# The end of a decoder layer: final norm with its weights multiplied in early, four roots at once and one correction for the last rows

## The chip, the cores and the metric

One core of a Trainium2 chip runs the whole program. The metric is the device time in microseconds, the median of several runs. All engines (PE the matmuls, DVE VectorE, ACT ScalarE, POOL GpSimd, SP which issues transfers) work through their own instruction queues in order and wait for one another by semaphores.

## What is computed

One layer of a decoder trunk over 1024 tokens of width 1024: three mixers of the tokens merged under gates, then a two-layer MLP, then a final RMS norm. The change lies in the last lines, after the second MLP product:

```python
def rms_norm(x, g):
    x32 = x.astype(jnp.float32)
    y = x32 * lax.rsqrt(jnp.mean(x32 * x32, axis=-1, keepdims=True) + EPS)
    return (y * g.astype(jnp.float32)).astype(x.dtype)
...
        hn = rms_norm(h, norm_mlp_g[l])
        up = jax.nn.relu(jnp.einsum('bsd,df->bsf', hn, w_mlp_up[l]))
        h = h + jnp.einsum('bsf,fd->bsd', up * up, w_mlp_down[l])
    return rms_norm(h, final_norm_g)
```

## The kernel before

The tokens lie in eight row chunks `H[0]` to `H[7]` of 128 rows and 1024 columns (tiles `a` in the profile); a chunk has two halves of 512 columns, `hsl(0)` and `hsl(1)`. The second MLP product is computed by a seven-product scheme: for each of `NJ` slices of the hidden width there are seven bursts `i` = 0 to 6, and each burst has four products `p` = 0 to 3 of 12 matmuls (float32 operands split in a high and a low part). `dn_product(n, p)` issues one product and its eviction (L1617): DVE adds the result in PSUM to a half of `H[c]`. In a slice, bursts 3 to 6 accumulate into the same four PSUM banks (`aux2`), so a product's partial sums are evicted four times. Which half is meant goes by the burst: `i` = 3 the left halves of `H[0..3]`, 4 their right halves, 5 the right halves of `H[4..7]`, 6 the left halves of `H[4..7]`.

The order of the instructions on each engine is the order in which the code is written (a manual schedule). Between the products `advance(dn)` issues a step that splits operands of a later burst: a cast on ACT (L132) and a subtraction on DVE (L133). The last such step stands behind product 2 of burst 4 of the last slice.

In the last slice (`final`) the norm is woven in from burst 3 on. Every evicted half is squared and summed by ACT (L1822) into a column `fs`. With burst 5 the rows `H[p]`, complete by then, get their root from `rsqrt_col` (L107 to L112: a first guess by integer arithmetic and three corrections, nine column operations on DVE, behind the addition L1787), and one DVE instruction (L1827) scales a whole row chunk by root and weights `fg`; SP sends it out in two halves. The right halves of `H[4..7]` are multiplied by the weights (L1825). With burst 6 the left halves are multiplied by the weights, on POOL for `p` < 3 and on DVE for the last (L1832); root and scaling of a chunk follow one product later: both halves by ACT (L1799, L1795), of the last chunk one by DVE (L1802). All output transfers are issued by SP (L1783).

Of the kernel before, what the change touches and what calls it, by code (L numbers as in the profile page):

```python
# [11 lines left out]
AF = mybir.ActivationFunctionType  # L12
ALU = mybir.AluOpType
# [3 lines left out]
P = 128  # L17
T = 1024
D = 1024
KD = D // P  # L20
NCH = T // P
HF = 512
EPS = 1e-6
# [13 lines left out]
def trunk_kernel(ctx: ExitStack, tc: tile.TileContext, x, norm_mix_g, w_in, b_gate, gmlp_ln_g, gmlp_ln_b,  # L37
# [4 lines left out]
    nc = tc.nc  # L42
    x, w_in, b_gate, out = x[0], w_in[0], b_gate[0], out[0]
# [24 lines left out]
    def nm(s):  # L68
        uid[0] += 1
        return f"{s}_{uid[0]}"  # L70

    def act(shape=(P, T), dt=F32):
        return pools[0].tile(list(shape), dt, tag="act", name=nm("a"))
# [7 lines left out]
    def sm(n, tag, dt=F32, bufs=None):  # L81
        return small.tile([P, n], dt, tag=tag, name=nm(tag), bufs=bufs)
# [3 lines left out]
    tt = nc.vector.tensor_tensor  # L86
    stt = nc.vector.scalar_tensor_tensor
    ts = nc.vector.tensor_scalar
    actv = nc.scalar.activation
    mm = nc.tensor.matmul  # L90

    def hsl(h):
        return slice(h * HF, h * HF + HF)
# [11 lines left out]
    def rsqrt_col(dst, v, scale, e):  # L105
        nh, r, q = sm(1, "rsq_v", bufs=2), sm(1, "rsq_r", bufs=2), sm(1, "rsq_q", bufs=2)
        ts(out=r, in0=v, scalar1=scale, scalar2=e, op0=ALU.mult, op1=ALU.add)  # L107
        ts(out=nh, in0=r, scalar1=-0.5, scalar2=None, op0=ALU.mult)
        ts(out=r.bitcast(I32), in0=r.bitcast(I32), scalar1=-0.5, scalar2=float(0x5F3759DF), op0=ALU.mult, op1=ALU.add)
        for i in range(3):  # L110
            stt(out=q, in0=r, scalar=nh, in1=r, op0=ALU.mult, op1=ALU.mult)  # L111
            stt(out=(dst if i == 2 else r), in0=q, scalar=1.5, in1=r, op0=ALU.add, op1=ALU.mult)  # L112
# [172 lines left out]
    with tc.manual_schedule():  # L285
# [29 lines left out]
        ss, rs = sm(NCH, "ss"), sm(NCH, "rsx")  # L315
# [8 lines left out]
        def row_scale(c, pool=False):  # L324
            if pool:
                nc.gpsimd.tensor_scalar(out=rows[c], in0=rows[c], scalar1=rs[:, c:c + 1], scalar2=0.0, op0=ALU.mult, op1=ALU.add)
            else:
                ts(out=rows[c], in0=rows[c], scalar1=rs[:, c:c + 1], scalar2=None, op0=ALU.mult)
# [13 lines left out]
        row_sum(0)  # L342
        row_root(0, 1)
        row_scale(0)
        wv0 = v_weights(0, (0,))
        xt[0] = transpose_rows(rows[0])
# [4 lines left out]
        x_low(xt[0], 0, 0)  # L351
        x_high(xt[0], 0, 1)
        row_scale(1)
        x_low(xt[0], 0, 1)
        v_start(0, range(0, 4))
# [9 lines left out]
        x_low(xt[1], 1, 0)  # L365
        row_root(2, 3)
        row_scale(2)
        x_low(xt[1], 1, 1)
        row_root(3, 4)
# [170 lines left out]
    queue, ready, pending = [], [], []  # L540
# [515 lines left out]
    for c in range(NCH):  # L1056
# [5 lines left out]
        rs = sm(1, "lrs")  # L1062
# [305 lines left out]
    H = []  # L1368
# [20 lines left out]
    with tc.manual_schedule():  # L1389
        for cp in range(NCH // 2):  # L1390
# [15 lines left out]
            for i in range(2):  # L1406
                h = H[2 * cp + i]
# [194 lines left out]
    def dn_product(n, p):  # L1602
        j, i = divmod(n, 7)
        if i < 3:
            if i == 0:
                main[j, "b2", p] = aux()
            ps = main[j, "b2", p] if i < 2 else aux()
        else:
            if i == 3:
                main[j, p] = aux2()  # L1610
            ps = main[j, p]
        u, w = OPS[n]
        lhs = [[u[part][kk][:, p * P:(p + 1) * P] for kk in range(4)] for part in range(2)]
        seventh(ps, lhs, w, i in (0, 2, 3))
        c, nb = {0: (p + 4, 1), 1: (p, 1), 2: (p, 0), 3: (p, 0), 4: (p, 1), 5: (p + 4, 1), 6: (p + 4, 0)}[i]
        h = H[c][:, hsl(nb)]
        tt(out=h, in0=ps, in1=h, op=ALU.add)  # L1617
        return c, nb

    def advance(gen):  # L1620
        next(gen, None)
# [23 lines left out]
    with tc.manual_schedule():  # L1645
# [125 lines left out]
        H = [None] * NCH  # L1771
        for c in (4, 5, 6, 7, 0, 1, 2, 3):
            H[c] = act()
            nc.scalar.dma_start(out=H[c], in_=h_d[c])
            if c == 7:
                dn_product(0, 0)
                prev.p4()
                prev.last_sum()
        sums, scaled = {}, {}
        roots = sm(NCH, "roots")  # L1780

        def out_row(c, nb, o):
            nc.sync.dma_start(out=out[c * P:(c + 1) * P, hsl(nb)], in_=o)  # L1783

        def row_scale(c):
            rs = roots[:, c:c + 1]
            tt(out=sums[c, 0], in0=sums[c, 0], in1=sums[c, 1], op=ALU.add)  # L1787
            rsqrt_col(rs, sums[c, 0], 1.0 / D, EPS)
            return rs

        def last_rows(c, rs, left):
            o = scaled[c]
            left(o[:, hsl(0)], rs)
            out_row(c, 0, o[:, hsl(0)])
            actv(o[:, hsl(1)], o[:, hsl(1)], AF.Identity, scale=rs)  # L1795
            out_row(c, 1, o[:, hsl(1)])

        def by_scalar(o, rs):
            actv(o, o, AF.Identity, scale=rs)  # L1799

        def by_vector(o, rs):
            ts(out=o, in0=o, scalar1=rs, scalar2=None, op0=ALU.mult)  # L1802

        waiting = None
        for n in range(NB):
            j, i = divmod(n, 7)
            final = j == NJ - 1
            if final and i == 3:
                fg = act()
                nc.scalar.dma_start(out=fg, in_=final_norm_g.partition_broadcast(P))  # L1810
            for p in range(NCH // 2):
                if n + p == 0:
                    continue
                c, nb = dn_product(n, p)
                advance(dn)
                if final and i == 3:
                    advance(dn)
                if not final or i < 3:
                    continue
                h = H[c][:, hsl(nb)]  # L1820
                sums[c, nb] = sm(1, f"fs{c}{nb}")
                actv(act()[:, :HF], h, AF.Square, accum_out=sums[c, nb])  # L1822
                if i == 5:
                    scaled[c] = act()
                    tt(out=scaled[c][:, hsl(1)], in0=h, in1=fg[:, hsl(1)], op=ALU.mult)  # L1825
                    rs, o = row_scale(p), act()
                    stt(out=o, in0=H[p], scalar=rs, in1=fg, op0=ALU.mult, op1=ALU.mult)  # L1827
                    for b in range(2):
                        out_row(p, b, o[:, hsl(b)])
                elif i == 6:  # L1830
                    eng = nc.gpsimd if p < 3 else nc.vector
                    eng.tensor_tensor(out=scaled[c][:, hsl(0)], in0=h, in1=fg[:, hsl(0)], op=ALU.mult)  # L1832
                    if waiting is not None:
                        last_rows(waiting, row_scale(waiting), by_scalar)
                    waiting = c
        last_rows(waiting, row_scale(waiting), by_vector)
# [1 line left out]
_INS = ['x', 'norm_mix_g', 'w_in', 'b_gate', 'gmlp_ln_g', 'gmlp_ln_b', 'gmlp_w_s', 'gmlp_b_s', 'lru_conv_w',  # L1838
        'lru_conv_b', 'lru_w_r', 'lru_b_r', 'lru_w_i', 'lru_b_i', 'lru_lambda', 'ssd_conv_w', 'ssd_conv_b',
# [25 lines left out]
```

## Time and profile before

| | |
|---|---|
| median of 3 runs | 1958.79 us (1957.18 to 1960.37) |
| span of the profiled execution | 1959.5 us (no separate time is given for it; the span is 0.7 us above the median) |
| granted TensorE clock, mean | 0.991 |
| PE busy | 1905.2 us, 97% |
| DVE busy | 1410.2 us, 72% |
| ACT busy | 1014.1 us, 52% |
| POOL busy | 259.3 us, 13% |

A line of the timeline has the start in us, the duration, the engine, the line of the kernel, the operation, output <- inputs, shapes and count; in square brackets stands how long the engine sat idle before it and what ended that. A line of groups has the busy time, then the mean ns of one. In the rows of groups and of the timeline buffer numbers are left out, so `a<-a,a` can be three tiles. Ends of matmuls are modelled.

### The profile page before, as it was taken

What the parts mean: (1) busy time and instruction counts of PE and PEld (TensorE: products, weight loads), DVE (VectorE), ACT (ScalarE), POOL (GpSimd) and SP (SyncE); (2) the same over time, 40 slices, a digit from 0 to 9 for tenths busy, and PEclk for the clock granted to TensorE, in tenths of its full rate; (3) what the DMA queues carried; (4) which work ended last, traced back from release to release, by engine and by line L of the source; (5) the groups of instructions that cost most, each with busy time, mean ns of one, the idle gap of its engine ahead of it and who ended that gap; (6) DMA issues with size and microseconds to landing.
All of it is one profiled execution on the core that took longest, in us unless ns stands there. A gap on an engine that the chain in (4) does not pass through costs nothing.

```text
span 1959.5 us, 23757 instructions
## 1 busy us (share of the span) xinstructions
PE 1905.2 (97%) x8928; PEld 1587.5 (81%) x8928; DVE 1410.2 (72%) x2039; ACT 1014.1 (52%) x1471; POOL 259.3 (13%) x355
## 2 busy tenths in 40 slices
PE   8999999999999999999999999998999999999996
PEld 7998878888887787878778887877788887888885
DVE  6585869788758767677777888248655567688787
ACT  6435959676534545454554544167555556243253
POOL 3112112122342010100010110000211110000000
PEclk9999999999999999999999999999999999999998
DMA  4346475576754343434497986331544448453532
GB/s 162 75 137 145 110 153 122 121 164 138 169 142 136 107 151 108 151 108 129 149 287 256 279 220 194 107 108 54 199 139 167 154 172 294 164 172 118 183 119 86
DMA packets 211015, 301.25 MB, mean 154 GB/s; under 512 B 13028, under 2 KB 125876, under 8 KB 210900
## 3 DMA queue, kind: packets, MB, share of 16 engines
q1 hardware_dynamic: 167348, 158.54, 26.4%
q0 software_dynamic: 34544, 119.69, 22.8%
q10 hardware_dynamic: 9008, 21.51, 3.1%
q8 instruction: 70, 1.15, 0.3%
q14 instruction: 45, 0.37, 0.1%
HBM read 195.75 MB, written 74.58 MB: 138 GB/s over the span
## 4 chain that ended last, share of the span: by engine, by line
PE 74%; DVE 9%; issue 6%; ACT 5%; DMA 5%; POOL 1%; ACTq 0%; POOLq 0%; DVEq 0%; SPq 0%
PE aux L487 39%; PE ps L564 14%; PE gps L487 10%; PE aux L257 4%; PE aux L1387 2%; PE aux L800 1%; DMA a<-acs_d 1%; DMA c<-yc_d 1%; ACT a L1436 1%; DMA raw<-in_w_in_dram 1%; PE aux L736 1%; PE aux L732 1%; DVE a L133 1%; DVE rsq_q L111 1%; ACT a L132 1%
## 5 line engine op out<-in xcount | busy, mean ns | idle before, releaser
L564 PE MATMUL ps<-xn,wh 128*128 128x512 f32 x1088 | 295.0, 392 | 0.0
L487 PE MATMUL aux<-b,b 128*128 128x512 f32 x1152 | 264.4, 389 | 1.0 <-DVE b L133 0.9
L487 PEld LDWEIGHTS aux<-b,b 128*128 128x128 f32 x1152 | 216.0, 188 | 47.0 <-DVE b L133 1.8
L564 PEld LDWEIGHTS ps<-xn,wh 128*128 128x128 f32 x1088 | 202.9, 188 | 42.2 <-issue 0.9
L487 PE MATMUL aux<-a,b 128*128 128x512 f32 x960 | 219.4, 389 | 0.0
L487 PEld LDWEIGHTS aux<-a,b 128*128 128x128 f32 x960 | 180.2, 188 | 37.4
L564 PE MATMUL ps<-xn,wl 128*128 128x512 f32 x544 | 168.2, 389 | 0.0
L487 PE MATMUL gps<-xn,wt 128*128 128x512 f32 x684 | 160.2, 392 | 2.1 <-DVE a L238 2.1
L487 PE MATMUL aux<-b,wt 128*128 128x512 f32 x672 | 156.9, 389 | 0.0
L487 PEld LDWEIGHTS gps<-xn,wt 128*128 128x128 f32 x684 | 129.4, 189 | 29.5 <-issue 2.5
L487 PEld LDWEIGHTS aux<-b,wt 128*128 128x128 f32 x672 | 126.1, 188 | 26.2
L132 ACT ACTIVATE b<-wt 128x1024 fp32r<-128x1024 f32 x88 | 90.8, 1052 | 86.4 <-DMA wt<-u_d 51.9
L133 DVE TENSOR_TENSOR wt<-a,wt 128x1024 fp32r<-128x1024 f32 x66 | 80.8, 1225 | 66.9 <-ACT wt L132 66.9
L564 PEld LDWEIGHTS ps<-xn,wl 128*128 128x128 f32 x544 | 102.1, 188 | 21.4
L133 DVE TENSOR_TENSOR b<-wt,b 128x1024 fp32r<-128x1024 f32 x88 | 107.1, 1218 | 15.8 <-ACT b L132 15.8
L1617 DVE TENSOR_TENSOR a<-aux,a 128x512 f32<-128x512 f32 x112 | 76.9, 687 | 50.2 <-PE aux L487 50.2
L133 DVE TENSOR_TENSOR a<-a,a 128x1024 fp32r<-128x1024 f32 (+1 forms) x68 | 66.6, 985 | 41.5 <-ACT a L132 41.5
L133 DVE TENSOR_TENSOR wt<-rt,wt 128x1024 fp32r<-128x1024 f32 x35 | 42.8, 1224 | 57.2 <-ACT wt L132 57.0
L132 ACT ACTIVATE a<-a 128x1024 fp32r<-128x1024 f32 (+1 forms) x68 | 55.9, 837 | 54.1 <-DVE a L1569 45.9
L487 PE MATMUL aux<-a,wt 128*128 128x512 f32 x336 | 78.7, 390 | 3.3 <-ACT a L1494 3.3
L487 PEld LDWEIGHTS aux<-a,wt 128*128 128x128 f32 x336 | 62.9, 188 | 17.2 <-ACT a L1494 4.2
L132 ACT ACTIVATE wt<-a 128x1024 fp32r<-128x1024 f32 x66 | 69.6, 1055 | 8.7 <-DVE a L515 8.3
(349 smaller groups left out, 3521.2 us busy)
## 6 DMA issues: line engine op xcount, KB each, us to landing
wt<-u_d SPq DMA_DIRECT2D x54, 512.0 KB
u_d<-a POOLq DMA_DIRECT2D x48, 512.0 KB, 5.3
raw<-in_w_in_dram SPq DMA_DIRECT2D x34, 512.0 KB
wl<-raw POOLq DMA_DIRECT2D x34, 512.0 KB, 5.1
g_d<-a POOLq DMA_DIRECT2D x24, 512.0 KB, 3.3
a<-g_d ACTq DMA_DIRECT2D x24, 512.0 KB
rt<-in_w_in_dram SPq DMA_DIRECT2D x19, 512.0 KB
a<-in_w_in_dram SPq DMA_DIRECT2D x19, 512.0 KB
```

The lines of the kernel that those rows point to most:

```text
L111: stt(out=q, in0=r, scalar=nh, in1=r, op0=ALU.mult, op1=ALU.mult)
L132: actv(dst_hi, src, AF.Copy)
L133: (eng or nc.vector).tensor_tensor(out=dst_lo, in0=src, in1=dst_hi.bitcast(F32), op=ALU.subtract)
L257: mm(ps[:, :nt], X.tok(a, k, c), wk[k][w], start=(k == 0 and i == 0), stop=(k == KD - 1 and i == 2))
L487: mm(ps, lhs[l][kk], rhs[r][kk], start=(new and n == 0), stop=(n == 11), skip_group_check=not new)
L564: mm(ps[:, hsl(h)], w[wi][:, k, :], a.rhs(ai, k, h), start=(n == 0), stop=(n == 3 * KD - 1))
L732: mm(yo[:, tok(i)], pv[c // 2][:, c % 2, j * P:(j + 1) * P], Cf[:, tok(c)], start=True, stop=True)
L736: mm(yi[64 * h:64 * h + 64, tok(i)], xdt[c // 2][:, c % 2, 2 * j + h, :], E[c // 2][:, c % 2, 2 * j + h, :], start=True, stop=True)
L800: mm(ps, w[wi][:, q * P:(q + 1) * P], S["xs"][half][ai], start=(n == 0), stop=(n == 2))
L1387: mm(ps, M.tok(a, k, c), wo[nb][k][w], start=(k == 0 and a + w == 0), stop=(k == KD - 1 and a == 1))
L1436: actv(Nf[th, k // 2][:, k % 2, (c % 4) * P:(c % 4 + 1) * P], ps[:, i * P:(i + 1) * P], AF.Identity, scale=g2c[:, KD + k:KD + k + 1])
L1617: tt(out=h, in0=ps, in1=h, op=ALU.add)
```

## The change

The weights are multiplied into the rows `H[0..3]` on DVE during burst 4 (`weigh`, L1790 of the new code), and into both halves of `H[4..7]` during bursts 5 and 6, all on DVE; POOL has no part in it any more. With the first product of burst 5 the roots of the four chunks `H[0..3]` are found together on 4 columns: mean (L1806, L1807), square root by ACT (L1808), then reciprocal and one correction by DVE (L1811 to L1815); ACT scales each chunk whole (L1802) and SP sends it in one transfer of 512 KB. For `H[4..7]`, the sum of squares of the half known first is turned into a bias column `known` (L1857); ACT takes the root of the other half's sum plus this bias (L1819), and DVE makes the reciprocal and one correction (L1823 to L1827). DVE scales the left half (L1795) and ACT the right (L1797), one product later. The very last transfer is issued by ACT.

```diff
+        def square_sum(c, nb):
+            actv(act()[:, :HF], H[c][:, hsl(nb)], AF.Square, accum_out=squares[c // half][nb][:, c % half:c % half + 1])
+        def weigh(c, nb):
...
+            tt(out=scaled[c][:, hsl(nb)], in0=H[c][:, hsl(nb)], in1=fg[:, hsl(nb)], op=ALU.mult)
+        def out_half(c, nb, eng, queue):
+            o, rs = scaled[c][:, hsl(nb)], root[:, c % half:c % half + 1]
+            if eng is nc.vector:
+                ts(out=o, in0=o, scalar1=rs, scalar2=None, op0=ALU.mult)
+            else:
+                actv(o, o, AF.Identity, scale=rs)
+            queue.dma_start(out=out[c * P:(c + 1) * P, hsl(nb)], in_=o)
+        def rows_first(p):
+            o = scaled[p]
+            actv(o, o, AF.Identity, scale=root[:, p:p + 1])
+            nc.sync.dma_start(out=out[p * P:(p + 1) * P, :], in_=o)
+        def roots_first():
+            tt(out=mean, in0=squares[0][0], in1=squares[0][1], op=ALU.add)
+            ts(out=mean, in0=mean, scalar1=1.0 / D, scalar2=EPS, op0=ALU.mult, op1=ALU.add)
+            actv(root, mean, AF.Sqrt)
+        def refine_first():
+            nc.vector.reciprocal(out=root, in_=root)
+            tt(out=step_, in0=root, in1=root, op=ALU.mult)
+            tt(out=step_, in0=step_, in1=mean, op=ALU.mult)
+            ts(out=step_, in0=step_, scalar1=-0.5, scalar2=1.5, op0=ALU.mult, op1=ALU.add)
+            tt(out=root, in0=root, in1=step_, op=ALU.mult)
+        def root_last(p):
+            q = slice(p, p + 1)
+            actv(root[:, q], squares[1][0][:, q], AF.Sqrt, scale=1.0 / D, bias=known[:, q])
+        def refine_last(p):
+            q = slice(p, p + 1)
+            stt(out=mean[:, q], in0=squares[1][0][:, q], scalar=1.0 / D, in1=known[:, q], op0=ALU.mult, op1=ALU.add)
+            ts(out=mean[:, q], in0=mean[:, q], scalar1=-0.5, scalar2=None, op0=ALU.mult)
+            nc.vector.reciprocal(out=root[:, q], in_=root[:, q])
+            stt(out=step_[:, q], in0=root[:, q], scalar=mean[:, q], in1=root[:, q], op0=ALU.mult, op1=ALU.mult)
+            stt(out=root[:, q], in0=step_[:, q], scalar=1.5, in1=root[:, q], op0=ALU.add, op1=ALU.mult)
...
-                h = H[c][:, hsl(nb)]
-                sums[c, nb] = sm(1, f"fs{c}{nb}")
-                actv(act()[:, :HF], h, AF.Square, accum_out=sums[c, nb])
-                if i == 5:
-                    scaled[c] = act()
-                    tt(out=scaled[c][:, hsl(1)], in0=h, in1=fg[:, hsl(1)], op=ALU.mult)
-                    rs, o = row_scale(p), act()
-                    stt(out=o, in0=H[p], scalar=rs, in1=fg, op0=ALU.mult, op1=ALU.mult)
-                    for b in range(2):
-                        out_row(p, b, o[:, hsl(b)])
+                square_sum(c, nb)
+                if i == 4:
+                    weigh(c, 0)
+                    weigh(c, 1)
+                elif i == 5:
+                    if p == 0:
+                        roots_first()
+                    weigh(c, 1)
+                    if p == 0:
+                        refine_first()
+                    rows_first(p)
                 elif i == 6:
-                    eng = nc.gpsimd if p < 3 else nc.vector
-                    eng.tensor_tensor(out=scaled[c][:, hsl(0)], in0=h, in1=fg[:, hsl(0)], op=ALU.mult)
-                    if waiting is not None:
-                        last_rows(waiting, row_scale(waiting), by_scalar)
-                    waiting = c
-        last_rows(waiting, row_scale(waiting), by_vector)
+                    if p == 0:
+                        ts(out=known, in0=squares[1][1], scalar1=1.0 / D, scalar2=EPS, op0=ALU.mult, op1=ALU.add)
+                    root_last(p)
+                    weigh(c, 0)
+                    if p:
+                        out_half(c - 1, 0, nc.vector, nc.sync)
+                        out_half(c - 1, 1, nc.scalar, nc.sync)
+                    refine_last(p)
+        out_half(NCH - 1, 0, nc.vector, nc.sync)
+        out_half(NCH - 1, 1, nc.scalar, nc.scalar)
```

On DVE, at product 2 of burst 6 (the left half of `H[6]`), stood the eviction and then the chain of the chunk before (`H[5]`): sum, mean, guess, three corrections; the weights of `H[6]` came from POOL.

```order
L1617 TENSOR_TENSOR a_1956_12961<-aux2_2292_14897,a_1956_12961 128x512
L1787 TENSOR_TENSOR fs50_2350_15193<-fs50_2350_15193,fs51_2327_15071 128x1
L107 TENSOR_SCALAR rsq_r_2358_15233<-fs50_2350_15193 128x1
L108 TENSOR_SCALAR rsq_v_2357_15232<-rsq_r_2358_15233 128x1
L109 TENSOR_SCALAR rsq_r_2358_15233<-rsq_r_2358_15233 128x1
L111 SCALAR_TENSOR_TENSOR rsq_q_2359_15234<-rsq_r_2358_15233,rsq_v_2357_15232 128x1
L112 SCALAR_TENSOR_TENSOR rsq_r_2358_15233<-rsq_q_2359_15234,rsq_r_2358_15233 128x1
...
L112 SCALAR_TENSOR_TENSOR roots_1963_13004<-rsq_q_2359_15234,rsq_r_2358_15233 128x1
```

The same place of DVE's queue in the new program (`fm` is `mean`, `fk` is `known`, `fr` is `root`, `fs_` is `step_`, `fs10` the sums of squares, `a_2282` the weights):

```order
L1617 TENSOR_TENSOR a_1956_12961<-aux2_2297_14902,a_1956_12961 128x512
L1790 TENSOR_TENSOR a_2328_15095<-a_1956_12961,a_2282_14848 128x512
L1795 TENSOR_SCALAR a_2326_15076<-a_2326_15076,fr_1968_13009 128x512
L1823 SCALAR_TENSOR_TENSOR fm_1967_13008<-fs10_1965_13006,fk_1970_13011 128x1
L1824 TENSOR_SCALAR fm_1967_13008<-fm_1967_13008 128x1
L1825 RECIPROCAL fr_1968_13009<-fr_1968_13009 128x1
L1826 SCALAR_TENSOR_TENSOR fs_1969_13010<-fr_1968_13009,fm_1967_13008 128x1
L1827 SCALAR_TENSOR_TENSOR fr_1968_13009<-fs_1969_13010,fr_1968_13009 128x1
```

A chain of ten has become one of five, now for the chunk just evicted; a weighing and a scaling of the previous chunk's half have come in.

On ACT, around the evictions of products 0 and 1 of burst 5, stood squares alone:

```order
L1822 ACTIVATE a_2319_15021,fs31_2318_15020<-a_1962_13002 128x512
L1822 ACTIVATE a_2321_15037,fs41_2320_15036<-a_1954_12957 128x512
L1822 ACTIVATE a_2328_15072,fs51_2327_15071<-a_1955_12959 128x512
L1822 ACTIVATE a_2335_15107,fs61_2334_15106<-a_1956_12961 128x512
L1822 ACTIVATE a_2342_15142,fs71_2341_15141<-a_1957_12963 128x512
```

There the new program has the table load and the four roots, and the scaling of the rows between the squares:

```order
L1785 ACTIVATE a_2321_15029,fs01_1964_13005<-a_1962_13002 128x512
L1785 ACTIVATE a_2323_15047,fs11_1966_13007<-a_1954_12957 128x512
L1808 ACT_TABLE_LOAD
L1808 ACTIVATE fr_1968_13009<-fm_1967_13008 128x4
L1802 ACTIVATE a_2312_14969<-a_2312_14969,fr_1968_13009 128x1024
L1785 ACTIVATE a_2325_15074,fs11_1966_13007<-a_1955_12959 128x512
L1802 ACTIVATE a_2316_14991<-a_2316_14991,fr_1968_13009 128x1024
L1785 ACTIVATE a_2327_15093,fs11_1966_13007<-a_1956_12961 128x512
```

This is the only table load from there to the end; the last one ahead of it, in both programs, stands with the mixers (L926). The scaling of whole rows has moved to ACT from DVE.

More of the change, by code (lines that the diff above doesn't have):

```diff
@@ L1778, in trunk_kernel @@
                 prev.last_sum()
[L1779 to L1804, printed above, removed]
+        half = NCH // 2
+        squares = [[sm(half, f"fs{th}{nb}") for nb in range(2)] for th in range(2)]
+        mean, root, step_, known = (sm(half, f"f{i}") for i in "mrsk")
+        scaled = {}
+        def square_sum(c, nb):
+            actv(act()[:, :HF], H[c][:, hsl(nb)], AF.Square, accum_out=squares[c // half][nb][:, c % half:c % half + 1])
@@ new lines, in weigh @@
+        def weigh(c, nb):
+            if c not in scaled:
+                scaled[c] = act()
+            tt(out=scaled[c][:, hsl(nb)], in0=H[c][:, hsl(nb)], in1=fg[:, hsl(nb)], op=ALU.mult)
[6 more added lines that the diff above has]
+            queue.dma_start(out=out[c * P:(c + 1) * P, hsl(nb)], in_=o)
@@ L1810, in trunk_kernel @@
                 nc.scalar.dma_start(out=fg, in_=final_norm_g.partition_broadcast(P))
-            for p in range(NCH // 2):
+            for p in range(half):
                 if n + p == 0:
```

## The prediction

> **What bounds the kernel now.** I read the page's head first, then busy time by stretch around the end of the program, then the timeline of its last 60 us. The stretches show busy us and instruction counts.
>
> ```profile
> span 1959.5 us, 23757 instructions
> PE 1905.2 (97%) x8928; PEld 1587.5 (81%) x8928; DVE 1410.2 (72%) x2039; ACT 1014.1 (52%) x1471; POOL 259.3 (13%) x355
> ...
> core 0: us, PE busy (x) PEld busy (x) DVE busy (x) ACT busy (x) POOL busy (x), PEclk, DMA share, GB/s
> ...
> 1912.00:1924.00 12.00, 12.00 (x55) 9.93 (x54) 7.88 (x10) 5.94 (x13) 0.00 (x0) 1.00 0.00 0
> 1924.00:1942.90 18.90, 18.89 (x84) 15.31 (x82) 17.36 (x53) 2.90 (x8) 0.00 (x0) 1.00 0.23 85
> 1942.90:1956.00 13.10, 0.00 (x0) 0.00 (x0) 11.33 (x46) 7.33 (x15) 3.76 (x3) 0.58 0.41 151
> ```
>
> PE is busy 97% of the span, but it stops at 1942.9, and 13.1 us follow in which only DVE (11.33 busy) and ACT work. Up to 1924 DVE has room (7.88 of 12); from there it is full. The change touches nothing ahead of about 1913. So its worth is read from this end, in which DVE is the bound.
>
> ```profile
> 1921.17 0.69 DVE L1617 TENSOR_TENSOR a<-aux,a 128x512 f32<-128x512 f32 x1 [0.90 <-PE aux L487]
> ...
> 1923.89 0.69 DVE L1617 TENSOR_TENSOR a<-aux,a 128x512 f32<-128x512 f32 x1 [2.03 <-PE aux L487]
> 1924.62 0.69 DVE L1825 TENSOR_TENSOR a<-a,a 128x512 f32<-128x512 f32 x1
> ...
> 1925.23 0.15 DVE L1787 TENSOR_TENSOR fs<-fs,fs 128x1 f32<-128x1 f32 x1
> 1925.42 0.15 DVE L107 TENSOR_SCALAR rsq_r<-fs 128x1 f32<-128x1 f32 x1
> ...
> 1925.98 0.22 DVE L111 SCALAR_TENSOR_TENSOR rsq_q<-rsq_r,rsq_v 128x1 f32<-128x1 f32 x1
> 1926.23 0.16 DVE L112 SCALAR_TENSOR_TENSOR rsq_r<-rsq_q,rsq_r 128x1 f32<-128x1 f32 x1
> ...
> 1927.33 1.28 DVE L1827 SCALAR_TENSOR_TENSOR a<-a,roots,a 128x1024 f32<-128x1024 f32 x1
> 1928.53 0.68 DVE L1617 TENSOR_TENSOR a<-aux,a 128x512 f32<-128x512 f32 x1
> ...
> 1931.85 11.04 PE L487 MATMUL aux<-b,b 128*128 128x512 f32 x48
> ...
> 1942.41 1.28 DVE L1617 TENSOR_TENSOR a<-aux,a 128x512 f32<-128x512 f32 x2
> 1943.13 0.63 ACT L1822 ACTIVATE a<-a 128x512 f32<-128x512 f32 x1 [3.90 <-DVE a L1617]
> 1943.23 2.49 POOL L1832 TENSOR_TENSOR a<-a,a 128x512 f32<-128x512 f32 x2 [296.30 <-DVE a L1617]
> 1943.66 0.19 ACT L1822 ACTIVATION_READ_ACCUMULATOR a<-a 128x1 f32 x1
> ...
> 1943.88 0.63 DVE L1787 TENSOR_TENSOR fs<-fs,fs 128x1 f32<-128x1 f32 x1 [0.19 <-ACT a L1822]
> ...
> 1945.11 0.63 DVE L111 SCALAR_TENSOR_TENSOR rsq_q<-rsq_r,rsq_v 128x1 f32<-128x1 f32 x1
> ...
> 1955.26 0.72 ACT L1795 ACTIVATE a<-a,roots 128x512 f32<-128x512 f32 x1 [0.58 <-DVE roots L112]
> 1955.26 0.49 DVE L1802 TENSOR_SCALAR a<-a,roots 128x512 f32<-128x512 f32 x1
> ```
>
> The evictions (L1617) at 1921.17 and 1923.89 both waited for PE: one product takes 2.72 us. Counted from there, the products of the last burst but one (i = 5) are ready at 1923.89, 1926.61, 1929.33 and 1932.05, those of the last (i = 6) at 1934.77, 1937.49, 1940.21 and 1942.93. But the second eviction of i = 5 comes at 1928.53, after a weighing, a chain of ten column operations (1925.23 to 1927.33, 2.10 us) and a scaled product of 1.28. Each such turn takes 4.64, so DVE falls back 1.9 us a product and evicts the first product of i = 6 at 1942.41, 7.6 us late. Four more chains follow; POOL's weighings stretch some of their members (0.63 in place of 0.15 and 0.22). The last output is ready at 1955.98, 13.05 us after the last product.
>
> **The change, part by part.** A "step" below is the time from one instruction's start to the next one's: eviction to a weighing that reads it 0.73 (1923.89 to 1924.62), weighing to the next 0.61, column operation 0.19, a column operation with a second column as scalar 0.25 (1925.98 to 1926.23).
>
> *The norm-weight products at i = 4.* Eight weighings of 0.69 move to where DVE had room, two behind each product of i = 4. With the splits (L133) still there, one turn is
>
> ```profile
> 1892.01 1.22 DVE L133 TENSOR_TENSOR b<-a,b 128x1024 fp32r<-128x1024 f32 x1
> 1893.14 1.22 DVE L1578 TENSOR_TENSOR a<-rt,a 128x1024 f32<-128x1024 f32 x1
> ```
>
> 0.60 + 1.13 + 0.73 + 0.61 = 3.07 against 2.72 (an independent successor starts 0.08 before its forerunner ends, as at 1925.23 and 1893.14). Started at 1913.62, DVE is 0.96, 1.31 and 1.67 us late at the next three products and evicts the first of i = 5 at 1924.90, 1.0 late. Nothing waits for that: burst i = 6 reads the last split only from 1931.85, and three other products (8.2 us) lie between two that use one bank of PSUM.
>
> *The four roots at i = 5.* Four chains of 2.10 and four L1827 (1.28) leave DVE: about 13.5 us. In come two column operations, one weighing a product, a wait for ScalarE's root, and five column operations. ScalarE must load a table first. Rows of the same kind elsewhere:
>
> ```profile
> 655.02 1.05 ACT L132 ACTIVATE wt<-a 128x1024 fp32r<-128x1024 f32 x1
> 656.09 1.28 ACT L973 ACT_TABLE_LOAD   x1
> 657.38 0.69 ACT L973 ACTIVATE x<-aux,eps 128x512 f32<-128x512 f32 x1
> ...
> L341 ACT ACTIVATE g2c<-aux 128x16 f32<-128x16 f32 x1 | 0.2, 184 | 3.3 <-PE aux L339 3.3
> ...
> L812 ACT ACTIVATE h<-h 128x512 f32<-128x512 f32 x16 | 10.1, 630 | 0.2
> ...
> L222 DVE RECIPROCAL a<-a 128x8 f32<-128x8 f32 x1 | 0.2, 203 | 0.0
> ...
> L1422 ACT ACTIVATE a<-a,rs 128x1024 f32<-128x1024 f32 x8 | 9.2, 1153 | 16.0 <-DVE rs L112 16.0
> ```
>
> The square behind the eviction of 1924.90 starts at 1925.67, the load at 1926.30, the root runs 1927.59 to 1927.78 (0.19; the 128x16 row is the nearest). DVE has been idle since 1926.58: a new wait of 1.2 us, with the eviction of the second product queued behind it. Reciprocal (between 0.15, the least DVE row, and 0.20 of the 128x8 row: 0.20) and four steps end at 1928.81. Then the products, at 1.34 each: evictions at 1928.81 (2.2 late), 1930.15 (0.8 late), 1932.05 (on time). DVE has caught up. On ScalarE a product costs square 0.63 and scaling 1.15, under 2.72; its last full-row scaling ends near 1935.0.
>
> The Trainium skill ("ScalarE: Activation LUTs", section "What ACT_TABLE_LOAD costs") gives 1283 ns for the load and another 1380 ns of drain for every switch of set. The load agrees with the 1.28 above. The drain does not: the load starts 0.02 after the instruction ahead ends, and the root 0.01 after the load. By the page the sum would be 0.7 us longer (rival 2), by the rows as it stands.
>
> *One correction at i = 6.* A chain falls from ten members to five. L1823 0.19, L1824 0.19, reciprocal 0.23, L1826 0.25, L1827 0.17: 1.03, each from its likeness above. ScalarE's root with a column as bias costs 0.25: the 0.19 plus the 0.06 by which L973, with such a bias, exceeds L812. It ends 1.8 us after the eviction starts (0.77 to the square, 0.73 for square and read-out), before the reciprocal wants it. One turn of DVE is eviction 0.72, weighing 0.61, scaling the previous rows' half 0.43, chain 1.03: 2.79 against PE's 2.72. The first product also carries L1857, and waits 0.1 us for its square; it ends at 1937.33, in time for the second. Lateness then grows 0.07 a product: 0.1 at the third, 0.20 at the fourth.
>
> *POOL.* Its three weighings move to DVE (in the turn above), and the stretching of the chains goes.
>
> **Sum.** From the last product ready (1942.93): lateness 0.20, eviction 0.72, weighing 0.61, scaling 0.43, chain 1.03, last scaling on ScalarE 0.72, together 3.71. The last output is ready at 1946.64, against 1955.98.
>
> ```profile
> 1954.09 0.33 SPq L1783 DMA_DIRECT2D out_dram<-a  x1
> ...
> 1955.77 0.81 SPq L1783 DMA_DIRECT2D out_dram<-a  x2
> ```
>
> *The output transfers.* From 1955.98 to the end 3.52 us passed, 0.27 of them because SP issued two transfers in turn; now ScalarE issues the last, which bounds the rest below by 3.25. From above: four 256 KB transfers went out from 1954.09 and all was over 5.41 later. The last four now begin at 1944.95, which gives 1950.36. I take 1950.2, between 1949.9 and 1950.4. The first rows go out at 1930 in pieces of 512 KB, under work. The gain is 1959.5 - 1950.2 = 9.3 us. The profiled span is 0.7 above the median of the three runs (1958.79); the difference taken off the median gives 1949.5.
>
> **The rivals.**
> 1. *The chain of i = 6 does not fit in PE's 2.72.* If all five members cost 0.25 and each turn waits 0.15 for ScalarE, a turn is 3.16 and the end comes 3 x 0.37 + 0.37 = 1.5 later: 1951.0. For it: five small operations with a hand-over in their midst are not in the trace. Against: the rows 0.15 to 0.22.
> 2. *The table switch stalls ScalarE for a second load's length.* The evictions of i = 5 fall back 1.3 further; ScalarE's queue is then 0.8 late at the first product of i = 6, and the turns of 2.79 give none of it back: 1950.2. The rows at 656 speak against it. The Trainium skill's page "ScalarE: Activation LUTs" (section "What ACT_TABLE_LOAD costs", as above) describes such a stall.
> 3. *The output transfers set the end.*
>
> ```profile
> GB/s 101 347 8 11 0 191 391 118 0 0 0 134 377 189 0 0 0 68 382 249 0 0 0 0 117 382 199 0 60 388 251 0 0 287 388 216 391 118 0 0
> ```
>
> At the 391 GB/s of that row (slices of 0.75 us from 1930) 256 KB take 0.67, so the last four take 2.7 us while they are issued within 1.8. If they also meet a 512 KB remainder, 1.3 is added: 1950.8.
> 4. *Slower: the matmuls' pace.* In the built program the small tiles shrink (17 padded to 32 bytes each become 8), so every tile of pools a and h lies 288 bytes lower for the whole run. Nothing in the trace prices that. The nearest rows are two groups of the same matmul on different tiles:
>
> ```profile
> L564 PE MATMUL ps<-xn,wh 128*128 128x512 f32 x1088 | 295.0, 392 | 0.0
> ...
> L564 PE MATMUL ps<-xn,wl 128*128 128x512 f32 x544 | 168.2, 389 | 0.0
> ```
>
> 3 in 389 over 1905 us would be 14.7 us either way: 1964 or 1935. The gain is gone at 9.3, that is 0.49% of pace; a slowdown of 0.2% needs 0.69%. Against it: groups whose tiles lie all over the memory differ by no more than this.
>
> **Chances.** A change of 0.2% (3.9 us) is about what a measurement of this kernel can tell from none. Forecast 0.58; rival 1 0.12; rival 2 0.08; rival 3 0.05; pace faster 0.05; pace slower 0.12, of which 0.07 ends within 0.2% and 0.05 beyond. Faster is 0.88, same 0.07, slower 0.05. The range: the low end 1946.5 is the forecast less the 1.6 us by which the lowest of three runs lies under the median, and 1.4 us for shorter members and a little pace; the high end 1955.0 is rival 1, the same 1.6, and 0.1% of pace, which is also the edge of no change.
>
> **What would show it.** In the profile after: DVE waits about 1.2 us for ScalarE once, at L1811; the evictions of i = 6 wait for PE again or are under 0.3 late; L1802 and the squares fit on ScalarE; from PE's end to the last scaling some 3.7 us. Wrong would be an eviction of i = 6 more than 1 us late, a second table load, a PE idle stretch in the last 30 us, or a PE busy time other than 1905.

## The result: slower, with the end of the program as forecast and PE late

The changed kernel takes 1964.04 us (median of 6 runs, 1963.61 to 1966.01) against 1957.95 before (6 runs): 1.0030 of the time, 95% interval 1.0020 to 1.0041. Forecast was 1949.5.

First the head of the page after the change, then its groups of the second MLP and the mixers' seven-product matmuls (L487). A row has busy us and the mean ns of one.

```profile
span 1962.5 us, 23708 instructions
PE 1919.7 (98%) x8928; PEld 1586.4 (81%) x8928; DVE 1403.1 (71%) x1997; ACT 1019.7 (52%) x1478; POOL 254.8 (13%) x352
...
L487 PE MATMUL aux<-b,b 128*128 128x512 f32 x1152 | 264.8, 390 | 0.8 <-DVE b L133 0.8
L487 PE MATMUL aux<-a,b 128*128 128x512 f32 x960 | 225.8, 396 | 0.0
L487 PE MATMUL aux<-b,wt 128*128 128x512 f32 x672 | 157.6, 390 | 0.0
L487 PE MATMUL aux<-a,wt 128*128 128x512 f32 x336 | 82.4, 402 | 3.3 <-ACT a L1494 3.3
```

The same four groups before:

```profile
L487 PE MATMUL aux<-b,b 128*128 128x512 f32 x1152 | 264.4, 389 | 1.0 <-DVE b L133 0.9
L487 PE MATMUL aux<-a,b 128*128 128x512 f32 x960 | 219.4, 389 | 0.0
L487 PE MATMUL aux<-b,wt 128*128 128x512 f32 x672 | 156.9, 389 | 0.0
L487 PE MATMUL aux<-a,wt 128*128 128x512 f32 x336 | 78.7, 390 | 3.3 <-ACT a L1494 3.3
```

As many matmuls as before keep PE busy for 1919.7 us in place of 1905.2, and the 14.5 us lie in some groups alone. The tiles `b` and `wt` lie where they lay; their groups cost what they cost within 1 ns (389 before, 390 after). The tiles `a` have moved by 288 bytes; groups that join them with `b` or `wt` now show 396 and 402. Counted from start to start in the traces, the 960 matmuls `a,b` come 226.7 ns apart on average before and 233.4 after. It shows far from the end too, more than 100 us ahead of any changed instruction; busy time in one stretch before, then after:

```profile
1700.00:1800.00 100.00, 100.00 (x443) 82.81 (x442) 79.30 (x86) 41.52 (x42) 0.00 (x0) 1.00 0.42 138
```

```profile
1700.00:1800.00 100.00, 100.00 (x434) 81.21 (x433) 75.79 (x82) 34.29 (x35) 0.00 (x0) 1.00 0.44 143
```

443 matmuls have become 434 in 100 us, at the same granted clock of 1.00. The end itself, from the timeline after the change:

```profile
1936.70 0.63 ACT L1785 ACTIVATE a<-a 128x512 f32<-128x512 f32 x1 [1.15 <-DVE fm L1806]
...
1937.23 0.18 ACT L1785 ACTIVATION_READ_ACCUMULATOR a<-a 128x1 f32 x1
1937.44 1.28 ACT L1808 ACT_TABLE_LOAD   x1
1938.73 0.20 ACT L1808 ACTIVATE fr<-fm 128x4 f32<-128x4 f32 x1
1938.97 0.18 DVE L1811 RECIPROCAL fr<-fr 128x4 f32<-128x4 f32 x1 [1.50 <-ACT fr L1808]
...
1944.11 11.06 PE L487 MATMUL aux<-b,b 128*128 128x512 f32 x48
1944.31 0.69 DVE L1617 TENSOR_TENSOR a<-aux,a 128x512 f32<-128x512 f32 x1 [1.38 <-PE aux L487]
...
1947.06 0.69 DVE L1617 TENSOR_TENSOR a<-aux,a 128x512 f32<-128x512 f32 x1 [1.33 <-PE aux L487]
...
1952.49 0.69 DVE L1617 TENSOR_TENSOR a<-aux,a 128x512 f32<-128x512 f32 x1
...
1955.21 0.69 DVE L1617 TENSOR_TENSOR a<-aux,a 128x512 f32<-128x512 f32 x1
1955.94 0.63 ACT L1785 ACTIVATE a<-a 128x512 f32<-128x512 f32 x1 [1.05 <-DVE a L1617]
...
1957.84 0.72 ACT L1797 ACTIVATE a<-a,fr 128x512 f32<-128x512 f32 x1 [0.24 <-DVE fr L1827]
...
1958.59 0.34 ACTq L1798 DMA_DIRECT2D out_dram<-a  x1
```

DVE waits for PE again in the last bursts, and the last eviction starts 0.03 us after PE's last matmul ends (1955.18); before the change, DVE was 7.6 us late at the first product of burst 6 and 6.9 at the last. From PE's end to the last scaling's end pass 3.39 us; they were 13.08. So 9.7 us were won behind PE's end, and PE ends 12.3 us later; with 0.4 us more for the last transfers, the span is 3.0 us longer (1962.5 against 1959.5). The medians differ by 6.1, because the profiled execution of before was a long one: in the runs with both figures the time is 1.7 us more than the span, so a span of 1959.5 stands for some 1961.2, 3.2 above the median of 1957.95.

### The profile page after: what moved, and what is told of

It is laid out like the page before. It is cut to its first block, busy times and chain, and to the rows that moved or that the text cites. A ratio compares the mean times of both kernels' runs of the same rounds, so it can differ in the third digit from the quotient of the medians.

```text
span 1962.5 us, 23708 instructions
## 1 busy us (share of the span) xinstructions
PE 1919.7 (98%) x8928; PEld 1586.4 (81%) x8928; DVE 1403.1 (71%) x1997; ACT 1019.7 (52%) x1478; POOL 254.8 (13%) x352
## 4 chain that ended last, share of the span: by engine, by line
PE 83%; DVE 6%; ACT 4%; issue 3%; DMA 3%; POOL 1%; ACTq 0%; SPq 0%; POOLq 0%; DVEq 0%
PE aux L487 43%; PE ps L564 16%; PE gps L487 13%; PE aux L257 4%; PE aux L1387 2%; PE aux L800 1%; ACT a L1436 1%; PE aux L736 1%; PE aux L732 1%; PE aux L712 1%; ACT a L132 1%; DVE a L133 0%; DMA yr_d<-h 0%; PE aux L847 0%; DVE b L133 0%
## 5 line engine op out<-in xcount | busy, mean ns | idle before, releaser
L564 PE MATMUL ps<-xn,wh 128*128 128x512 f32 x1088 | 295.1, 392 | 0.0
L487 PE MATMUL aux<-b,b 128*128 128x512 f32 x1152 | 264.8, 390 | 0.8 <-DVE b L133 0.8
L487 PEld LDWEIGHTS aux<-b,b 128*128 128x128 f32 x1152 | 216.0, 188 | 47.4 <-DVE b L133 1.6
L564 PEld LDWEIGHTS ps<-xn,wh 128*128 128x128 f32 x1088 | 202.9, 188 | 42.5 <-issue 0.7
L487 PE MATMUL aux<-a,b 128*128 128x512 f32 x960 | 225.8, 396 | 0.0
L487 PEld LDWEIGHTS aux<-a,b 128*128 128x128 f32 x960 | 180.3, 188 | 43.6
L564 PE MATMUL ps<-xn,wl 128*128 128x512 f32 x544 | 168.5, 390 | 0.0
L487 PE MATMUL gps<-xn,wt 128*128 128x512 f32 x684 | 158.8, 389 | 2.1 <-DVE a L238 2.1
L487 PE MATMUL aux<-b,wt 128*128 128x512 f32 x672 | 157.6, 390 | 0.0
L487 PEld LDWEIGHTS gps<-xn,wt 128*128 128x128 f32 x684 | 128.2, 188 | 29.0 <-issue 2.5
L487 PEld LDWEIGHTS aux<-b,wt 128*128 128x128 f32 x672 | 126.2, 188 | 27.1
L564 PEld LDWEIGHTS ps<-xn,wl 128*128 128x128 f32 x544 | 102.1, 188 | 21.5
L487 PE MATMUL aux<-a,wt 128*128 128x512 f32 x336 | 82.4, 402 | 3.3 <-ACT a L1494 3.3
L487 PEld LDWEIGHTS aux<-a,wt 128*128 128x128 f32 x336 | 64.1, 191 | 19.5 <-ACT a L1494 4.1
```

Of the source, the lines that this page charges most:

```text
L487: mm(ps, lhs[l][kk], rhs[r][kk], start=(new and n == 0), stop=(n == 11), skip_group_check=not new)
L564: mm(ps[:, hsl(h)], w[wi][:, k, :], a.rhs(ai, k, h), start=(n == 0), stop=(n == 3 * KD - 1))
```

## The experiments

Each is timed against the kernel before on the same chip. `SPACER` is the number of float32 columns of an unused tile among the small ones. "Moved" tiles are those of the pools that stand behind the small tiles in memory: `a`, `h`, `c` and `lw`, and the constants. Unmoved are `w` (`wt`), `raw` and `ident` in front of them, and `xn` and `b` at the far end.

**The changed kernel at the old addresses.**

```diff
-SPACER = 32
+SPACER = 104
```

> The changed kernel with the spacer tile enlarged by 288 bytes, so that every tile of the pools behind the small one lies where it lay before the change; nothing else differs. Theory A (the move of those tiles by 288 bytes slowed the matmuls whose two operands lie on either side of it from 227 to 235 ns; the new end of the program does what was forecast): matmuls back at 227 ns in every group, PE ends near 1943 us of the span, time 1949 to 1950 us. Theory B (the new code itself slows PE, by its load on ScalarE and VectorE or otherwise): 1964 us, PE end near 1955.

Measured: 1949.29 us (5 runs, 1947.09 to 1950.77), 0.9951 of before (0.9937 to 0.9964). Its page and group:

```profile
span 1948.0 us, 23708 instructions
PE 1903.6 (98%) x8928; PEld 1585.9 (81%) x8928; DVE 1402.7 (72%) x1997; ACT 1019.3 (52%) x1478; POOL 255.5 (13%) x352
...
L487 PE MATMUL aux<-a,b 128*128 128x512 f32 x960 | 219.4, 389 | 0.0
...
1929.68 11.04 PE L487 MATMUL aux<-b,b 128*128 128x512 f32 x48
...
1943.39 0.72 ACT L1797 ACTIVATE a<-a,fr 128x512 f32<-128x512 f32 x1 [0.24 <-DVE fr L1827]
```

72 unused columns, and PE is back at 1903.6 us with the same instructions as in the changed kernel. Theory B falls. In every group of `L487` with 512 columns the median step from start to start is 227 ns again; in the changed kernel it was 232 to 235 in the groups that join a moved with an unmoved tile. From PE's end (1940.72) to the last scaling (1944.11) pass 3.39 us. PE ends 2.2 us earlier than in the profile before, and is as much earlier already after 7000 of the 8928 matmuls (1501.1 against 1503.3), far ahead of the change.

**The kernel before, moved by 32 bytes.**

```diff
-SPACER = 32
+SPACER = 40
```

> The kernel before with the spacer tile 32 bytes larger and nothing else, so that the tiles of the pools behind it move up by 32 bytes: with respect to the unmoved tiles they lie as in the changed kernel, 32 bytes off a multiple of 64. Theory A in the form that the offset modulo 64 decides: matmuls with one moved and one unmoved operand at 235 ns, PE end 12 us later, time about 1970 us. Theory B: 1958 us, no change.

Measured: 1974.11 us (4 runs), 1.0078 of before (1.0064 to 1.0092). Eight unused columns in an otherwise untouched program cost 15.6 us, 4 more than theory A's "about 1970":

```profile
PE 1921.2 (97%) x8928; PEld 1586.0 (80%) x8928; DVE 1411.0 (72%) x2039; ACT 1014.8 (51%) x1471; POOL 259.6 (13%) x355
...
L487 PE MATMUL aux<-a,b 128*128 128x512 f32 x960 | 225.8, 395 | 0.0
```

**Moved by 64 bytes, and the changed kernel moved to -256.**

```diff
-SPACER = 32
+SPACER = 48   # the kernel before
```

> The kernel before with the spacer tile 64 bytes larger. Theory A, modulo 64: no change, 1958 us, all groups at 227 ns. Theory A in the other form, that the exact distance between the tiles counts (their distance modulo 512 is changed): 1965 to 1972 us.

```diff
-SPACER = 32
+SPACER = 40   # the changed kernel
```

> The changed kernel with the spacer tile 32 bytes larger, so that the moved tiles lie 256 bytes below their place in the kernel before, a multiple of 64. Theory A, modulo 64: as with the old addresses, 1949 to 1950 us. If the exact distance counts: between 1950 and 1964 us. Theory B: 1964 us.

Measured: 1967.72 us (4 runs; 1.0046, 1.0032 to 1.0060) for the first, 1949.79 us (4 runs; 0.9954, 0.9940 to 0.9968) for the second. The group in the first, then in the second:

```profile
L487 PE MATMUL aux<-a,b 128*128 128x512 f32 x960 | 221.7, 391 | 0.0
```

```profile
L487 PE MATMUL aux<-a,b 128*128 128x512 f32 x960 | 219.4, 389 | 0.0
```

A multiple of 64 is not enough, so theory A in its form "modulo 64" falls; nor does the exact distance count, since -256 is as good as 0. Both forms that were written down beforehand miss one of the two runs.

**Moved by 128 bytes.**

```diff
-SPACER = 32
+SPACER = 64   # the kernel before
```

> The kernel before with the spacer tile 128 bytes larger. So far matmuls on one moved and one unmoved tile took 227 ns for moves of 0 and -256 bytes, 229 for 64, 234 to 235 for 32 and -288. If a multiple of 128 is enough: 227 ns and 1958 us. If it takes 256: 229 ns or more, 1964 to 1972 us.

Measured: 1973.93 us (4 runs; 1.0077, 1.0063 to 1.0091).

```profile
L487 PE MATMUL aux<-a,b 128*128 128x512 f32 x960 | 225.7, 395 | 0.0
```

128 does not do either, and it costs 2 us more than the range that was expected for that case. Start to start, the group `a,b` stands at 226.7 ns for moves of 0 and -256, 229.1 for 64, 233.2 for 128, 233.4 for 32 and for -288. No profile shows an address. By the sizes of the pools in the kernel before, the small tiles take 1280 bytes, so `a` lies a multiple of 256 from `wt`, and not of 512; that `b` too lies a multiple of 256 from them is inferred from its full pace.

**Everything moved together.** A small tile is added to the first pool and one to the pool at the far end, so that no operand keeps its old place modulo 256 and all keep their distances.

```diff
-SPACER = 32
+SPACER = 40
+    base.tile([P, 56], F32, name="lift")
+    edge = ctx.enter_context(tc.tile_pool(name="edge", bufs=1, side="right"))
+    edge.tile([P, 8], F32, name="edge")
```

> The changed kernel with every pool of matmul operands moved with respect to the kernel before: the pools in front of the small one and those behind it and those at the far end all lie 32 bytes below a place of before, modulo 256 (moves of +224, -32 and -32 bytes). If the place of a tile by itself decides (a start of 224 modulo 256, as everything had it before): 234 ns and 1964 us or more, since now no tile has it. If the distance between the two tiles of a matmul, modulo 256, decides: 227 ns and 1949 to 1950 us.

Measured: 1949.87 us (4 runs; 0.9957, 0.9940 to 0.9974); the lines of this kernel are 3 higher.

```profile
L490 PE MATMUL aux<-a,b 128*128 128x512 f32 x960 | 219.4, 389 | 0.0
```

It is the distance between the two tiles that decides, modulo 256 as far as these six distances tell, and not a tile's own place.

Which two tiles these are can be read from the traces of the changed kernel and of its run at the old addresses, since their matmuls pair off one by one. (Of the two inputs in a row, the first is streamed and the second holds the weights. Counted are matmuls with 512 columns that follow one another without a pause.) Inside a long run of one group the weights of a matmul and of the next lie in the same pool; at the seams between groups they need not. 62 matmuls with both tiles unmoved stand ahead of one whose weights lie in a moved tile: the next start comes 6.6 ns later than at the old addresses. 31 stand ahead of one that streams a moved tile but has unmoved weights: 0.2 ns. 51 matmuls with both tiles moved stand ahead of unmoved weights: 8.1 ns; 451 ahead of moved ones: 1.7 on average, 0 in the median. So what counts is the tile that a matmul streams and the tile that holds the weights of the next one, not the matmul's own two.

**The first half of the change alone**, at the old addresses (fewer small tiles have gone, so `SPACER` is 48): chunks `H[0..3]` as in the changed kernel, `H[4..7]` as before. Of the difference to the changed kernel:

```diff
+                if i < 5:
+                    square_sum(c, nb)
+                else:
+                    h = H[c][:, hsl(nb)]
+                    sums[c, nb] = sm(1, f"fs{c}{nb}")
+                    actv(act()[:, :HF], h, AF.Square, accum_out=sums[c, nb])
...
                 elif i == 6:
-                    if p == 0:
-                        ts(out=known, in0=squares[1][1], scalar1=1.0 / D, scalar2=EPS, op0=ALU.mult, op1=ALU.add)
-                    root_last(p)
-                    weigh(c, 0)
...
+                    eng = nc.gpsimd if p < 3 else nc.vector
+                    eng.tensor_tensor(out=scaled[c][:, hsl(0)], in0=h, in1=fg[:, hsl(0)], op=ALU.mult)
+                    if waiting is not None:
+                        last_rows(waiting, row_scale(waiting), by_scalar)
+                    waiting = c
+        last_rows(waiting, row_scale(waiting), by_vector)
```

> Old addresses. Of the change only the part for the first four row chunks (weights at burst 4, four roots at once, rows scaled by ScalarE); the last four rows keep the old chains and POOL's weighings. From the terms of the prediction: VectorE is on time at burst 5, each old turn at burst 6 takes eviction 0.6, chain 2.1 and some 0.4 of stretching by POOL, 3.1 against 2.72; behind the last product follow lateness 1, eviction 0.6, weighing 0.6, two chains 4.2 and the scaling 0.7: 7.1 us in place of 13.05. Time 5.9 below the kernel before, 1952.6 us. If the two halves shared the 9.3 us by their numbers of instructions, it would be 1953 to 1954.

Measured: 1953.67 us (7 runs, 1951.39 to 1956.50; 0.9974, 0.9963 to 0.9985). The time lies 1.1 us above what was expected and where the rival had it, but seven runs spread over 5 us; the profile decides. From PE's end to the last scaling pass 6.94 us, of 7.1 expected. In its timeline PE's end, the evictions of burst 6, the stretched member of a chain and the last scaling:

```profile
1928.22 11.04 PE L487 MATMUL aux<-b,b 128*128 128x512 f32 x48
...
1931.14 0.69 DVE L1617 TENSOR_TENSOR a<-aux,a 128x512 f32<-128x512 f32 x1 [1.30 <-PE aux L487]
1933.86 0.69 DVE L1617 TENSOR_TENSOR a<-aux,a 128x512 f32<-128x512 f32 x1 [2.03 <-PE aux L487]
...
1935.22 0.77 DVE L111 SCALAR_TENSOR_TENSOR rsq_q<-rsq_r,rsq_v 128x1 f32<-128x1 f32 x1
...
1936.99 0.68 DVE L1617 TENSOR_TENSOR a<-aux,a 128x512 f32<-128x512 f32 x1
...
1940.07 0.68 DVE L1617 TENSOR_TENSOR a<-aux,a 128x512 f32<-128x512 f32 x1
...
1945.47 0.72 ACT L1844 ACTIVATE a<-a,roots 128x512 f32<-128x512 f32 x1 [0.60 <-DVE roots L112]
```

DVE is on time at the first two products of burst 6 and then falls back 0.4 us a product (turns of 3.13 and 3.08), so it is 0.8 us late at the last.

**The last half alone**, at the old addresses (`SPACER` is 48). Of the difference to the changed kernel:

```diff
+                if i < 5:
+                    sums[c, nb] = sm(1, f"fs{c}{nb}")
+                    actv(act()[:, :HF], H[c][:, hsl(nb)], AF.Square, accum_out=sums[c, nb])
+                else:
+                    square_sum(c, nb)
+                if i == 5:
                     weigh(c, 1)
-                elif i == 5:
-                    if p == 0:
-                        roots_first()
-                    weigh(c, 1)
-                    if p == 0:
-                        refine_first()
-                    rows_first(p)
+                    rs, o = row_scale(p), act()
+                    stt(out=o, in0=H[p], scalar=rs, in1=fg, op0=ALU.mult, op1=ALU.mult)
+                    for b in range(2):
+                        out_row(p, b, o[:, hsl(b)])
                 elif i == 6:
```

> Old addresses. Of the change only the part for the last four row chunks (root by ScalarE, one correction); the first four keep their old chains on VectorE at burst 5. The first product of burst 6 is then evicted as late as before, near 1942.4, and four turns of 2.79 and one scaling of 0.7 follow: last output ready near 1954.3, against 1955.98. Time 1.7 below the kernel before, 1956.8 us; the two halves alone give 7.6 us, together 9.3. A rival, that the halves are independent and each gives its share: 1954.

Measured: 1956.97 us (11 runs, 1955.07 to 1959.17; 0.9991, 0.9982 to 1.0000). The time alone hardly tells it from no change; the profile does: from PE's end to the last scaling 11.47 us, 1.6 under the 13.08 of before, as expected, but on another way. PE's end, the evictions of burst 6 and the last scaling in its timeline:

```profile
1927.18 11.04 PE L487 MATMUL aux<-b,b 128*128 128x512 f32 x48
...
1937.75 0.68 DVE L1617 TENSOR_TENSOR a<-aux,a 128x512 f32<-128x512 f32 x1
...
1939.20 1.28 ACT L1818 ACT_TABLE_LOAD   x1
...
1940.83 0.16 DVE L1824 RECIPROCAL fr<-fr 128x1 f32<-128x1 f32 x1 [1.26 <-ACT fr L1818]
...
1941.36 0.68 DVE L1617 TENSOR_TENSOR a<-aux,a 128x512 f32<-128x512 f32 x1
1943.85 0.69 DVE L1617 TENSOR_TENSOR a<-aux,a 128x512 f32<-128x512 f32 x1
1946.35 0.69 DVE L1617 TENSOR_TENSOR a<-aux,a 128x512 f32<-128x512 f32 x1
...
1948.97 0.72 ACT L1796 ACTIVATE a<-a,fr 128x512 f32<-128x512 f32 x1 [0.24 <-DVE fr L1826]
```

The turns are 3.61, 2.49 and 2.50 us, where 2.79 each were expected. DVE comes late from the old turns of burst 5, so nothing here waits for PE; the first turn holds the wait for ScalarE's table load, 1.26 us on the path, and the shorter turns behind it make up for most of that. The halves alone take 6.1 and 1.6 us from the stretch behind PE's end, both together 9.7, which is 1.9 more than their sum (before rounding). The lateness of DVE at the last eviction accounts for it. Before, it was 6.9 us; the last half alone makes it 8.1, 1.2 worse, which is about the wait for the table load; the first half alone leaves 0.8, since its old turns are longer than PE's product; with both halves it is nothing, since the load then lies in burst 5 under PE's work and the turns fit. That the load is what costs the last half its 1.2 us is read from the profile; no run has that half without it.

**The table loaded early**, the changed kernel at the old addresses.

```diff
+                if i == 4 and p == 2:
+                    actv(root, squares[0][0], AF.Sqrt)
```

> Old addresses, the whole change, and one more square root on four columns behind the square of product 2 of burst 4 (its result is overwritten), so that the table is loaded where ScalarE has room. By the forecast the wait of 1.2 us at the first reciprocal is caught up before burst 6: the wait shrinks to nothing and the time stays that of the changed kernel at old addresses, 1949.3 us within 0.5. The rival, that a stall of the table switch reaches the end: 0.6 to 1.3 us less, 1948.0 to 1948.7.

Measured: 1948.44 us (5 runs, 1947.64 to 1952.57; 0.9955, 0.9943 to 0.9968). By its median this lies outside what was expected and where the rival had it. But the runs spread over 5 us, and the intervals of this and of the first experiment (0.9951) overlap almost wholly, so the time does not choose; the profile does. The load now lies in burst 4, and the reciprocal waits for nothing:

```profile
1917.54 1.28 ACT L1846 ACT_TABLE_LOAD   x1
...
1922.33 0.18 DVE L1811 RECIPROCAL fr<-fr 128x4 f32<-128x4 f32 x1
...
1928.39 11.04 PE L487 MATMUL aux<-b,b 128*128 128x512 f32 x48
...
1942.09 0.72 ACT L1797 ACTIVATE a<-a,fr 128x512 f32<-128x512 f32 x1 [0.23 <-DVE fr L1827]
```

From PE's end to the last scaling pass 3.38 us, against 3.39 with the late load: that wait was free. The span is 1.3 us shorter than in the first experiment because PE is that much earlier already after 8800 matmuls (1910.25 against 1911.55), ahead of the added instruction.

## Why the prediction was wrong

*What bounds the end, and the sum.* Right. The stretch from the last product ready, 0.03 us behind PE's end, to the last output was forecast to fall from 13.05 to 3.71 us and fell to 3.36. At the old addresses, where nothing else differs, the time is 1949.29 us; 1949.5 was forecast. That they agree to 0.2 is partly luck: this stretch came out 0.35 us shorter than forecast and the transfers behind it 0.4 longer, and the two errors cancel.

*Terms.* Lateness at the last product: none, not 0.20, since the turn of burst 6 is no longer than PE's 2.72 (1952.49 to 1955.21). Its chain is shorter: at the last product it took 0.90 us from L1823's start to the scaling's (1956.94 to 1957.84) against 1.03, mostly because the reciprocal starts 0.07 us behind L1824, whose result it does not read; 0.19 was taken. ScalarE's root with a bias took 0.29 against 0.25, and hides. The wait at the first reciprocal was 1.50 us against 1.2 and cost nothing, as said. The table load stood 0.03 us behind the instruction ahead and 0.01 ahead of the root: no second stall, so rival 2 did not come. Nor did rival 1, since no turn of burst 6 was longer than PE's product.

*The transfers.* Mis-sized by 0.4: from the last scaling to the end of the span passed 3.9 us in the changed kernel (1958.56 to 1962.5) and at the old addresses (1944.11 to 1948.0) alike, 3.55 were taken. That they run together closer than before, as in rival 3, is a guess that was not tried; the first half alone, whose last transfers SP issues as before, shows 3.8.

*The step that failed* is the pace of the matmuls, rival 4. The sum leaves PE's work as it was, 1905 us busy; the tiles' move by 288 bytes is priced in the rival alone, which got a chance of 0.12, of which 0.05 beyond 0.2%. Measured, PE was busy 14.5 us longer with the same matmuls and ended 12.3 later, and the same program at the old addresses takes 14.8 us less: the gain of 9.3 was there and the move cost more. "A PE busy time other than 1905" was one of the prediction's own signs of being wrong.

The ground for the low chance was that "groups whose tiles lie all over the memory differ by no more than this". That row could not speak for it: before the change every group of these matmuls has a median step of 227 ns, so none showed a distance at which the pace suffers. The two rows taken as bounds (392 and 389 of L564) do not differ by their tiles' places either: after the change they read 392 and 390, and their median step is 227 ns in both. So it was luck that the price of 14.7 us, 3 ns in 389 on all of PE's 1905 us, came so near: what happened was some 7 ns on about 2300 of the 8928 matmuls. The right reading was that the change left the one set of distances that the trace knows, and that the trace said nothing of others. A resource without a bound that is busy for 97% of the span should have kept far more than 0.12, and the old addresses should have been named as the condition of the forecast.

## What to carry to other kernels

Compare the addresses of two builds before comparing their times: a change that only adds or drops a few small tiles can move every operand behind them. Where PE bounds the kernel, try to keep the tiles that meet in successive matmuls at the same place modulo 256 bytes, if need be with an unused tile. In this kernel the four moves by something else than a multiple of 256 cost 9 to 16 us in 1960, as much as the whole change gains or more; other shapes and types were not tried. When a stretch behind the last matmul is shortened, shorten the earlier turns too: a late engine carries its arrears to the end, and a table load that an early turn hides comes onto the path in a late one.

## What the runs showed of the hardware

A float32 matmul of 128x512 comes every 226.7 ns when the tile that it streams and the tile with the next one's weights lie a multiple of 256 bytes apart, 229.1 at 64, 233.2 to 233.4 at 32, 128 and -288: up to 3%, on some 2300 of the 8928 matmuls; in the stretch shown above the granted clock was 1.00 in both kernels. The seams between groups show that it is the current matmul's stream against the next one's weights. Where in the chip the two meet, no run here shows.
